# Key, value and query products of two heads as units of 512 and 384 moving columns in a decoder layer

## The chip, the core and the metric

The kernel runs on one core of one Trainium2 chip. The time is device microseconds of one execution. An execution is also profiled: each engine (TensorE is PE, its weight loads PEld, VectorE DVE, ScalarE ACT, GpSimd POOL, SyncE SP) has its instructions recorded with start and length, and the span runs from the first to the last of them.

## The reference

One layer of a hybrid decoder: a normalised and modulated input goes through one large projection, then a recurrent branch and an attention branch with compressed queries and keys run side by side, both are gated by silu, and an output product is added to the input. There are 512 tokens, 2048 model columns and 8 heads. Cut to what matters here:

```
h = rms_norm(x) * (1 + scale) + shift
xr, gr, qc, kvc, kr, ga = split(h @ w_in)              # qc, kvc: 512 columns each
y_rnn = rg_lru_branch(xr, ...) * silu(gr)
q  = (rms_norm(qc,  q_a_norm)  @ w_uq ).reshape(B, S, 8, 128 + 64)    # nope, rope
kv = (rms_norm(kvc, kv_a_norm) @ w_ukv).reshape(B, S, 8, 128 + 128)   # k nope, v
q_nope, k_nope = rms_norm(q_nope), rms_norm(k_nope)    # each head by itself
q_pe = apply_rope(rms_norm(q_pe)); k_pe = apply_rope(rms_norm(kr))
p = softmax(causal((q_nope . k_nope + q_pe . k_pe) / sqrt(192)))
y_att = (p @ v) * silu(ga)
x = x + gate * (concat(y_rnn, y_att) @ w_out)
```

## The kernel before

All matrix products are made in float32 precision from two parts: an operand is split into a high part in a reduced float32 format (a copy on ACT, `act(hi, src, AF.Copy)`) and the rest as low part (a subtraction on DVE), and a product is three matmuls: high by high, high by low, low by high. `wload` (line 192) does this for weights: SP issues the load of a tile into a raw buffer (`wraw`), ACT writes `whi`, DVE writes `wlo`. In the stage of interest there are 6 raw buffers and 3 each of `whi` and `wlo` (`NARROW`, line 30).

The work runs in stages. First come the modulation and the input projection in four chunks of its 2048 rows (tile `pp`, lines 508 to 554), with the recurrent branch beside the last chunk. Of the last chunk, the 8 column blocks of the attention gates (slots `pj24` to `pj31`) are left over. The stage behind it, from about 360 us on, is the attention. It is written as generators that are advanced tick by tick in `ticks` (line 1096):

- `produce(g)` makes q, k and v of the two heads of group g (g = 0 to 3);
- `attend(g)` makes the scores (`sc`), the softmax, the transposes of the probabilities (`tp`) and the product with v (`op`) for the same two heads;
- `fillers` (line 1037) are matmuls that depend on neither: the 8 left-over projection blocks (`pp`, in two loads each), then output products over heads that are done (`oa`).

In each run of `ticks`, `produce(g + 1)` stands beside `attend(g)`, and fillers are strewn between by a quota. This sets priorities. The order within each engine is then fixed at build time by a scheduler that goes by these priorities and by an estimate of when operands are ready; only SP's order is the written one. On the chip every engine takes its instructions strictly in that order, so a matmul whose operand is late holds all that are queued behind it.

`produce` before makes four products per group. `qpe` (line 840) makes the rotary part of q for two heads with the weights as stationary operand and the 512 tokens as moving columns: 12 matmuls of 512 columns into tile `uqp`, a copy, and four transposes (`tqp`, line 851) that bring the tokens into the partitions. Then `unit` (line 786) is used three times, for the other part of q (`wqn`), for k (`wuk`) and for v (`wuv`): a block of 128 tokens is the stationary operand, and 256 columns of weights of two heads move.

```
for b in range(2):
    wh, wl = wload(a[name][g][:, b * S:(b + 1) * S], S)
    for i in range(NT):
        o = pb[i // 2][:, (i % 2) * 256:(i % 2 + 1) * 256]
        for k in (2 * b, 2 * b + 1):
            mm(o, xh[k][:, t], wh[:, c], ...)   # then xh by wl, xl by wh
```

So a load of 512 columns (two of the four row blocks k) serves all four token blocks, 24 matmuls, and a unit has two PSUM banks with two token blocks each. All units share banks 0 and 1 in turn (`BANKS`, kind `u`). `nope` (line 802) takes a whole unit: copies out of both banks (`kt`), sums of squares (`jk`, `hs`), the inverse root on POOL (`rsq`, line 227), the scaling, transposes (`tq`) and the split of the result into `qT` or `kT`. `val` (line 833) copies v into `vt`. The gates' silu is taken in one batch behind the last left-over projection block (lines 1043 to 1046).

Of the kernel before, what the change touches and what calls it, by code (L numbers as in the profile page):

```python
# [12 lines left out]
F32 = mybir.dt.float32  # L13
F32R = mybir.dt.float32r
BF16 = mybir.dt.bfloat16
# [67 lines left out]
def body(ctx, nc, tc, a):  # L83
# [695 lines left out]
    def produce(g):  # L779
# [6 lines left out]
        def unit(name, xh, xl):  # L786
            pb = [bank("u", "u" + name) for _ in range(2)]
            for b in range(2):
                wh, wl = wload(a[name][g][:, b * S:(b + 1) * S], S)
                for i in range(NT):  # L790
                    t = slice(i * P, (i + 1) * P)
                    o = pb[i // 2][:, (i % 2) * 256:(i % 2 + 1) * 256]
                    for k in (2 * b, 2 * b + 1):
                        c = slice((k % 2) * 256, (k % 2 + 1) * 256)
                        mm(o, xh[k][:, t], wh[:, c], k == 0 and i % 2 == 0, False, skip_group_check=True)
                        mm(o, xh[k][:, t], wl[:, c], False, False, skip_group_check=True)
                        mm(o, xl[k][:, t], wh[:, c], False, k == 3, skip_group_check=True)
                if b == 0:
                    yield None
            yield pb  # L800

        def nope(pb, which, grow, dst):
            kt = [p3.tile([P, S], F32, tag="kt", name="kt", bufs=2) for _ in range(2)]
            s = p3.tile([P, 2, 4], F32, tag="hs", name="hs", bufs=2)
            for u in range(2):
                act(kt[u], pb[u], AF.Copy)
            for u in range(2):
                for q in range(4):
                    jk = p3.tile([P, P], BF16, tag="jk", name="jk")
                    act(jk, kt[u][:, q * P:(q + 1) * P], AF.Square, accum_out=s[:, u, q:q + 1])  # L810
            s3 = s.rearrange("p u (i h) -> p (u i) h", h=2)
            rb_ = lambda f: rl[:, which, f, :].rearrange("p (i o) -> p i o", o=1).broadcast_to([P, NT, 2])
            s8 = s.rearrange("p u q -> p (u q)")
            tt(s3, s3, rb_(1), ALU.mult)
            rsq(s8, s8, 1.0 / P, 8)
            tt(s3, s3, rb_(0), ALU.mult)
            yield
            for u in range(2):
                for q in range(4):
                    c = slice(q * P, (q + 1) * P)  # L820
                    stt(kt[u][:, c], kt[u][:, c], s[:, u, q:q + 1], row[:, grow:grow + P], ALU.mult, ALU.mult)
                tp = bank("tq", "tq")
                for d in range(2):
                    for i2 in range(2):
                        q = 2 * i2 + d
                        PE.transpose(tp[:, d * 256 + i2 * P:d * 256 + (i2 + 1) * P], kt[u][:, q * P:(q + 1) * P], ident)  # L826
                for d in range(2):
                    sl = slice(u * 256, (u + 1) * 256)
                    act(dst[d][:, 0, sl], tp[:, d * 256:(d + 1) * 256], AF.Copy)
                    tt(dst[d][:, 1, sl], tp[:, d * 256:(d + 1) * 256], dst[d][:, 0, sl].bitcast(F32), ALU.subtract)  # L830
                yield

        def val(pb):
            for i in range(NT):
                for d in range(2):
                    c0 = (i % 2) * 256 + d * P
                    act(vt4[d][:, i], pb[i // 2][:, c0:c0 + P], AF.Copy, scale=rl[:, 0, 0, i:i + 1])
            yield

        def qpe():  # L840
            wh, wl = wload(a["wqp"][g], S)
            ps = bank("u", "uqp")
            for k in range(4):
                c = slice(k * P, (k + 1) * P)
                mm3(ps, wh[:, c], wl[:, c], qh[k], ql[k], k == 0, k == 3)
            qs = p3.tile([P, S], F32, tag="qa", name="qs")
            act(qs, ps, AF.Copy)
            yield
            tp = bank("tq", "tqp")
            for i in range(NT):  # L850
                PE.transpose(tp[:, i * P:(i + 1) * P], qs[:, i * P:(i + 1) * P], ident)
            o = p3.tile([P, S], F32, tag="qb", name="qo")
            act(o, tp, AF.Square)
# [8 lines left out]
            tt(o8, tp.rearrange("p (n c) -> p n c", n=8), s.rearrange("p (n o) -> p n o", o=1).broadcast_to([P, 8, 64]),  # L862
# [22 lines left out]
        q = qpe()  # L885
        next(q, None)
        pipe.append(q)
        prods.append(q)
        yield
        for name, xh, xl, fin in (("wqn", qh, ql, lambda pb: nope(pb, 1, R_QN, qT)),  # L890
                                  ("wuk", kvh, kvl, lambda pb: nope(pb, 0, R_KN, kT)), ("wuv", kvh, kvl, val)):
            for pb in unit(name, xh, xl):
                if pb is not None:
                    f = fin(pb)
                    next(f, None)
                    pipe.append(f)
                    prods.append(f)
                yield
# [259 lines left out]
def _layout(x, c, positions, w_ada, b_ada, w_in, conv_w, conv_b, w_rg_a, b_rg_a, w_rg_x, b_rg_x, lru_lambda,  # L1158
# [30 lines left out]
    uk = w_ukv[0].reshape(2, 2, P, 4, 2, 2, P)  # L1189
    t = uk.transpose(3, 0, 2, 1, 5, 4, 6)  # L1190
    d["wuk"] = con(t[:, :, :, :, 0].transpose(0, 2, 1, 3, 4, 5)).reshape(4, P, 1024)
    d["wuv"] = con(t[:, :, :, :, 1].transpose(0, 2, 1, 3, 4, 5)).reshape(4, P, 1024)
    uq = w_uq[0].reshape(2, 2, P, 4, 2, 192).transpose(3, 0, 2, 1, 4, 5)
    d["wqn"] = con(uq[..., 0:128].transpose(0, 2, 1, 3, 4, 5)).reshape(4, P, 1024)
    uq2 = w_uq[0].reshape(4, P, 4, 2, 192).transpose(2, 1, 0, 3, 4)
    d["wqp"] = con(uq2[..., 128:192]).reshape(4, P, 512)
# [32 lines left out]
```

## Time and profile before

| | |
|---|---|
| median of 3 runs | 726.15 us (726.0 to 728.82) |
| the profiled execution's own time | 725.46 us |
| its span | 723.7 us |
| TensorE busy, matmuls | 718.7 us, 3608 |
| VectorE busy, instructions | 525.6 us, 945 |
| ScalarE busy, instructions | 354.2 us, 729 |
| granted TensorE clock | 1.00 |
| HBM read, written | 123.11 MB, 4.19 MB |

A row of a group gives line, engine, operation, output and inputs, shapes, count, then busy time and mean length of one, then the engine's idle time ahead of it and who ended most of it. A row of the timeline gives start, length, engine, line, operation, tiles, shape and count, and in brackets the idle time before it and its releaser. The chain is the work that ended last, followed back from the end: at each step to what released it, or to the instruction before it on its engine. All helpers for matmuls, copies and two-operand arithmetic are one line each (123, 88, 116), so tiles' names tell the groups apart. Matmuls overlap: the listed length of one is longer than the distance to the next one's start.

### The profile page before, as it was taken

The page shows a single profiled execution, that of the slowest core. Times are in us where ns is not written, and L with a number is a line of the kernel's source. Part 1 is how long each engine was busy: PE and PEld are TensorE (multiplying, and loading weights), DVE is VectorE, ACT ScalarE, POOL GpSimd, SP SyncE. Part 2 cuts the span into 40 slices and gives each one's busy share as a digit, 9 for nine tenths or more (in the row PEclk, how much of TensorE's full clock was granted, in tenths as well). Part 3 has the DMA queues.
Part 4 walks back from the last instruction along what each step waited for, and adds up shares of the span by engine and source line. Part 5 has one row for each costly group of instructions (what it writes and reads, how often), then busy time and mean ns, then how long its engine had stood idle before and what let it go on. Part 6 is the DMA issues. An engine that isn't in the chain of part 4 may idle for free.

```text
span 723.7 us, 10053 instructions
## 1 busy us (share of the span) xinstructions
PE 718.7 (99%) x3608; PEld 596.0 (82%) x3608; DVE 525.6 (73%) x945; ACT 354.2 (49%) x729; POOL 29.4 (4%) x34
## 2 busy tenths in 40 slices
PE   9999999999999999999999999999999999999998
PEld 4688888888888888888898898898888887888886
DVE  2867999998998889888755566567686786683232
ACT  7277222222233589884455578587465534222221
POOL 0000000000000000001011011111020100000000
PEclk9999999999999999999999999999999999999999
DMA  8998777877613321232342225213334685974330
GB/s 303 408 401 317 297 275 270 352 262 271 241 36 101 108 89 69 90 102 77 93 140 95 81 77 186 71 47 132 125 124 141 219 290 191 318 264 171 115 95 29
DMA packets 46145, 127.95 MB, mean 177 GB/s; under 512 B 5516, under 2 KB 9484, under 8 KB 42512
## 3 DMA queue, kind: packets, MB, share of 16 engines
q1 hardware_dynamic: 39040, 106.35, 41.3%
q10 hardware_dynamic: 7056, 20.97, 8.3%
q8 instruction: 28, 0.46, 0.3%
q14 instruction: 21, 0.17, 0.1%
HBM read 123.11 MB, written 4.19 MB: 176 GB/s over the span
## 4 chain that ended last, share of the span: by engine, by line
PE 99%; DVE 0%; ACT 0%; issue 0%
PE pp L123 48%; PE oa L123 24%; PE sc L123 4%; PE uwuv L123 3%; PE uwqn L123 3%; PE uwuk L123 3%; PE op L123 2%; PE junk_ps L123 2%; PE uqp L123 2%; PE tp L926 1%; PE pk L123 1%; PE tq L826 1%; PE pi L123 1%; PE pr L123 1%; PE tqe L881 0%; PE m_ps L123 0%
## 5 line engine op out<-in xcount | busy, mean ns | idle before, releaser
L123 PE MATMUL pp<-h,whi 128*128 128x512 f32 x992 | 241.1, 390 | 0.0
L88 ACT ACTIVATE whi<-wraw 128x512 fp32r<-128x512 f32 (+4 forms) x172 | 127.0, 741 | 227.7 <-PE pp L123 98.9
L123 PEld LDWEIGHTS pp<-h,whi 128*128 128x128 f32 x992 | 185.1, 188 | 38.3 <-issue 0.4
L116 DVE TENSOR_TENSOR wlo<-wraw,whi 128x512 fp32r<-128x512 f32 (+4 forms) x172 | 141.4, 824 | 72.0 <-ACT whi L88 33.9
L123 PE MATMUL pp<-h,wlo 128*128 128x512 f32 x496 | 126.7, 390 | 0.0
L123 PEld LDWEIGHTS pp<-h,wlo 128*128 128x128 f32 x496 | 92.9, 188 | 19.2
L123 PE MATMUL oa<-yh,whi 128*128 128x512 f32 (+1 forms) x260 | 100.9, 393 | 0.1
L123 PE MATMUL oa<-yl,whi 128*128 128x512 f32 (+1 forms) x260 | 101.0, 389 | 0.0
L116 DVE TENSOR_TENSOR pj<-pp,pj 128x512 f32<-128x512 f32 x96 | 65.0, 689 | 16.6 <-PE pp L123 15.9
L123 PE MATMUL oa<-yh,wlo 128*128 128x512 f32 (+1 forms) x260 | 71.2, 390 | 0.0
L277 DVE CUSTOM_DVE_ANT_0 ada<-ada,cb,vec 128x2048 f32<-128x2048 f32 (+1 forms) x31 | 69.6, 2247 | 1.5 <-DMA ada<-in_ada 1.5
L123 PEld LDWEIGHTS oa<-yl,whi 128*128 128x128 f32 x260 | 49.0, 188 | 9.3 <-DVE yl L116 0.2
L123 PEld LDWEIGHTS oa<-yh,whi 128*128 128x128 f32 x260 | 48.9, 188 | 9.4 <-ACT yh L88 0.3
L123 PEld LDWEIGHTS oa<-yh,wlo 128*128 128x128 f32 x260 | 48.0, 188 | 9.5
L123 PE MATMUL sc<-kT,qT 128*128 128x128 f32 (+3 forms) x96 | 22.5, 331 | 0.0
L918 DVE TENSOR_REDUCE nm<-sc 128x1 f32<-128x128 f32 (+3 forms) x32 | 15.5, 487 | 8.0 <-PE sc L123 7.9
L229 POOL TENSOR_TENSOR hs<-hs,mhalf 128x8 f32<-128x8 f32 x12 | 21.2, 1768 | 1.0
L88 ACT ACTIVATE pr<-sc,nm 128x128 f32<-128x128 f32 (+3 forms) x32 | 16.7, 522 | 9.1 <-DVE nm L918 9.0
L123 PE MATMUL uwuv<-whi,kvt 128*128 128x256 f32 x80 | 20.8, 284 | 0.0
L123 PE MATMUL uwqn<-whi,kvt 128*128 128x256 f32 x80 | 20.7, 286 | 0.0
L277 DVE CUSTOM_DVE_ANT_0 ada<-ada,cbo,modh 128x1024 f32<-128x1024 f32 x16 | 20.5, 1281 | 0.0
L277 DVE CUSTOM_DVE_ANT_0 ada<-ada,cbo,vec 128x1024 f32<-128x1024 f32 x16 | 20.5, 1280 | 0.0
(234 smaller groups left out, 995.8 us busy)
## 6 DMA issues: line engine op xcount, KB each, us to landing
ada<-in_ada SPq DMA_DIRECT2D x28, 1024.0 KB, 7.0
ada<-in_ada ACTq DMA_DIRECT2D x32, 512.0 KB, 5.1
wraw<-in_wout SPq DMA_DIRECT2D x59, 256.0 KB, 3.6
wraw<-in_win SPq DMA_DIRECT2D x22, 512.0 KB, 6.2
wraw<-in_win SPq DMA_DIRECT2D x24, 448.0 KB, 3.2
wraw<-in_win SPq DMA_DIRECT2D x16, 384.0 KB, 5.6
xtok<-in_xtok SPq DMA_DIRECT2D x8, 512.0 KB, 6.6
xo<-in_x SPq DMA_DIRECT2D x16, 256.0 KB, 5.0
```

The costliest lines, as they stand in the source:

```text
L88: return A.activation(out=out, in_=in_, func=func, **kw)
L116: return V.tensor_tensor(out=o, in0=x, in1=y, op=op)
L123: return PE.matmul(out=out, lhsT=lhsT, rhs=rhs, start=start, stop=stop, **kw)
L229: G.tensor_tensor(out=out, in0=out, in1=mhalf[:, :n], op=ALU.pow)
L277: ttr_last[0] = V.tensor_tensor_reduce(out=t, in0=t, in1=cv, op0=ALU.mult, op1=ALU.add, scale=1.0, scalar=vec[:, C_BADA + j:C_BADA + j + 1 ...
L826: PE.transpose(tp[:, d * 256 + i2 * P:d * 256 + (i2 + 1) * P], kt[u][:, q * P:(q + 1) * P], ident)
L918: V.tensor_reduce(out=nm, in_=sp[:, :n], axis=AX.X, op=ALU.max, negate=True)
L926: PE.transpose(tp[:, j * P:(j + 1) * P], pr[:, j * P:(j + 1) * P], ident)
```

## The change

Of the two products of k and v, one is made per group: `wkv`, in which a row block's weights for k and v of both heads stand side by side as 512 moving columns. Both parts of q become one product `wq` with 384 moving columns, 256 for the part without rotation and 128 for the rotary part, so that the rotary part comes out with the tokens in the partitions too and its transposes go. A unit now runs over two pairs of token blocks (u = 0, 1), one bank per token block. A load holds one row block k (384 or 512 columns); for u = 0 four are loaded in the order 0, 1, 2, 3, of which the last two stay split in their buffers, and for u = 1 the order is 3, 2, 1, 0, so that 1 and 0 are loaded again. Within a row block the four matmuls with the high weights come first, then the two with the low ones (for the very first two row blocks of group 0 the high ones of both come first). `nope` and `val` work on one pair of token blocks, and so run twice as often on half as much; their copies out of a bank are 256 or 128 columns wide. `qpe` reads the copy `qs` instead of transposes. A group thus loads 12 tiles (6 of 384 columns, 6 of 512) instead of 7 of 512. `produce` has 8 steps instead of 7, which `ticks` now counts with. The silu of the gates is taken in two batches of four, behind the fifth and the eighth left-over block. The weights are laid out for this on the host ahead of the launch, as they were before.

```diff
-        def unit(name, xh, xl):
-            pb = [bank("u", "u" + name) for _ in range(2)]
-            for b in range(2):
-                wh, wl = wload(a[name][g][:, b * S:(b + 1) * S], S)
...
+        def unit(name, n, xh, xl, fin):
+            held = {}
+
+            def piece(pb, u, ks, kn, ph):
+                k = ks[kn]
+                if k not in held:
+                    held[k] = wload(a[name][g][:, k * n:(k + 1) * n], n)
+                wh, wl = held[k]
+                for i in range(2):
+                    o, t = pb[i][:, :n], cols(2 * u + i)
+                    if ph:
+                        mm(o, xh[k][:, t], wl[:, :n], False, kn == 3)
+                    else:
+                        mm(o, xh[k][:, t], wh[:, :n], kn == 0, False)
+                        mm(o, xl[k][:, t], wh[:, :n], False, False)
+                if ph and u == 0 and kn < 2:
+                    del held[k]
+
             for u in range(2):
+                pb = [bank("u", "u" + name) for _ in range(2)]
+                ks = (0, 1, 2, 3) if u == 0 else (3, 2, 1, 0)
+
+                first = g == 0 and u == 0 and name == "wq"
+                for kn, ph in ((0, 0), (1, 0), (0, 1), (1, 1)) if first else ((0, 0), (0, 1), (1, 0), (1, 1)):
+                    piece(pb, u, ks, kn, ph)
+                yield
+                for kn in (2, 3):
+                    for ph in range(2):
+                        piece(pb, u, ks, kn, ph)
+                for f in fin(pb, u):
+                    next(f, None)
...
+        def nope(pb, u, which, grow, dst):
+            kt = p3.tile([P, S], F32, tag="kt", name="kt", bufs=2)
+            s = p3.tile([P, 4], F32, tag="hs", name="hs", bufs=2)
+            for i in range(2):
+                act(kt[:, i * 256:(i + 1) * 256], pb[i][:, 0:256], AF.Copy)
...
+        def val(pb, u):
+            for i in range(2):
                 for d in range(2):
...
+                    c0 = 256 + d * P
+                    act(vt4[d][:, 2 * u + i], pb[i][:, c0:c0 + P], AF.Copy, scale=rl[:, 0, 0, 2 * u + i:2 * u + i + 1])
+            yield
+
+        def qrope(pb, u):
+            if u == 0:
+                qs.append(p3.tile([P, S], F32, tag="qs", name="qs"))
+            for i in range(2):
+                act(qs[0][:, cols(2 * u + i)], pb[i][:, 256:384], AF.Copy)
+            yield
...
         def qpe():
-            wh, wl = wload(a["wqp"][g], S)
-            ps = bank("u", "uqp")
...
-            for i in range(NT):
-                PE.transpose(tp[:, i * P:(i + 1) * P], qs[:, i * P:(i + 1) * P], ident)
             o = p3.tile([P, S], F32, tag="qb", name="qo")
-            act(o, tp, AF.Square)
+            act(o, qs[0], AF.Square)
...
+        def qfin(pb, u):
+            fs = [qrope(pb, u), nope(pb, u, 1, R_QN, qT)]
+            return fs + [qpe()] if u else fs
+
+        yield from unit("wq", 384, qh, ql, qfin)
+        yield from unit("wkv", 512, kvh, kvl, lambda pb, u: [nope(pb, u, 0, R_KN, kT), val(pb, u)])
...
-            if n == 7:
-                for mm_ in MORDER[24:]:
+            if n in (4, 7):
+                for mm_ in MORDER[24:28] if n == 4 else MORDER[28:]:
...
-            want = -(-7 * (s + 1) // n) if prod is not None else 0
+            want = -(-8 * (s + 1) // n) if prod is not None else 0
```

The order on PE shows the shapes. Before, at the start of k of group 1 (the tiles' numbers tell instances apart; `kvt0`, `lat21` and `kvt1` are parts of the latent of k and v for row blocks 0 and 1):

```order
L123 MATMUL uwuk_3979<-whi_3983,kvt0_1840 128x256
L123 MATMUL uwuk_3979<-wlo_3984,kvt0_1840 128x256
L123 MATMUL uwuk_3979<-whi_3983,kvt0_1840 128x256
L123 MATMUL uwuk_3979<-whi_3983,lat21_2412 128x256
L123 MATMUL uwuk_3979<-wlo_3984,lat21_2412 128x256
L123 MATMUL uwuk_3979<-whi_3983,kvt1_1841 128x256
```

Now, at the start of k and v of group 1, for the two banks `uwkv_4009` and `uwkv_4010`:

```order
L123 MATMUL uwkv_4009<-whi_4013,kvt0_1840 128x512 x2
L123 MATMUL uwkv_4009<-wlo_4014,kvt0_1840 128x512
L123 MATMUL uwkv_4009<-whi_4025,lat21_2412 128x512
L123 MATMUL uwkv_4009<-whi_4025,kvt1_1841 128x512
L123 MATMUL uwkv_4010<-whi_4013,kvt0_1840 128x512 x2
```

Where one weight tile served two row blocks and 24 matmuls, each row block now has a tile of its own (`whi_4013`, `whi_4025`) and six matmuls for this pair of token blocks.

The second place on PE is in group 0, between the two halves of q. `whi_3131` and `whi_3143` (row blocks 2 and 3) are the two that stay for the second half, whose first bank is `uwq_3204`; `pp_3172` is a left-over projection block in two loads, `whi_3175` and `whi_3220`:

```order
L123 MATMUL pp_3172<-h12_1441,whi_3175 128x512 x2
L123 MATMUL uwq_3103<-wlo_3144,lat19_2716 128x384
L123 MATMUL uwq_3104<-wlo_3144,lat19_2716 128x384
L123 MATMUL pp_3172<-h9_1117,wlo_3176 128x512
L123 MATMUL pp_3172<-h10_1185,wlo_3176 128x512
L123 MATMUL pp_3172<-h11_1327,wlo_3176 128x512
L123 MATMUL pp_3172<-h12_1441,wlo_3176 128x512
L123 MATMUL pp_3172<-h13_1570,whi_3220 128x512 x2
L123 MATMUL pp_3172<-h14_1684,whi_3220 128x512 x2
L123 MATMUL pp_3172<-h15_1798,whi_3220 128x512 x2
L123 MATMUL uwq_3204<-whi_3143,lat19_2716 128x384
L123 MATMUL uwq_3204<-whi_3143,kvt4_1844 128x384
```

With two of three high buffers held, the projection's second tile takes the buffer that its first one leaves behind the row at the top; six matmuls lie between that row and its own first use.

The third place, also on PE, is the passage from q to k and v in group 0. `uwq_3204` and `uwq_3205` are the banks of q's second half; `uwkv_3368` takes the bank of `uwq_3204`:

```order
L123 MATMUL uwq_3204<-wlo_3268,kvt2_1842 128x384
L123 MATMUL uwq_3205<-wlo_3268,kvt2_1842 128x384
L123 MATMUL pp_3234<-h13_1570,wlo_3314 128x512
L123 MATMUL pp_3234<-h14_1684,wlo_3314 128x512
L123 MATMUL pp_3234<-h15_1798,wlo_3314 128x512
L123 MATMUL uwkv_3368<-whi_3372,kvt0_1840 128x512 x2
L123 MATMUL uwkv_3368<-wlo_3373,kvt0_1840 128x512
```

Four matmuls stand between the last one into the bank and the next use of it, which waits for two copies on ACT.

More of the change, by code (lines that the diff above doesn't have):

```diff
@@ L784, in produce @@
         grp[g] = (kT, qT, qp, vt4)
-        def unit(name, xh, xl):
-            pb = [bank("u", "u" + name) for _ in range(2)]
-            for b in range(2):
-                wh, wl = wload(a[name][g][:, b * S:(b + 1) * S], S)
-                for i in range(NT):
[L791 to L800, printed above, removed]
@@ L802, in nope @@
-        def nope(pb, which, grow, dst):
-            kt = [p3.tile([P, S], F32, tag="kt", name="kt", bufs=2) for _ in range(2)]
-            s = p3.tile([P, 2, 4], F32, tag="hs", name="hs", bufs=2)
-            for u in range(2):
[L806 to L813, printed above, removed]
+        def unit(name, n, xh, xl, fin):
[14 more added lines that the diff above has]
+                    del held[k]
+            for u in range(2):
+                pb = [bank("u", "u" + name) for _ in range(2)]
[9 more added lines that the diff above has]
+                    next(f, None)
+                    pipe.append(f)
+                    prods.append(f)
+                yield
@@ new lines, in nope @@
+        def nope(pb, u, which, grow, dst):
[3 more added lines that the diff above has]
+                act(kt[:, i * 256:(i + 1) * 256], pb[i][:, 0:256], AF.Copy)
+            for q in range(4):
+                jk = p3.tile([P, P], BF16, tag="jk", name="jk")
+                act(jk, kt[:, q * P:(q + 1) * P], AF.Square, accum_out=s[:, q:q + 1])
+            s3 = s.rearrange("p (i h) -> p i h", h=2)
+            rb_ = lambda f: rl[:, which, f, 2 * u:2 * u + 2].rearrange("p (i o) -> p i o", o=1).broadcast_to([P, 2, 2])
@@ L814, in nope @@
             tt(s3, s3, rb_(1), ALU.mult)
-            rsq(s8, s8, 1.0 / P, 8)
+            rsq(s, s, 1.0 / P, 4)
             tt(s3, s3, rb_(0), ALU.mult)
             yield
[L818 to L822, printed above, removed]
-                for d in range(2):
[L824 to L837, printed above, removed]
-            yield
-        def qpe():
-            wh, wl = wload(a["wqp"][g], S)
-            ps = bank("u", "uqp")
[L843 to L851, printed above, removed]
+            for q in range(4):
+                c = slice(q * P, (q + 1) * P)
+                stt(kt[:, c], kt[:, c], s[:, q:q + 1], row[:, grow:grow + P], ALU.mult, ALU.mult)
@@ new lines, in nope @@
+            tp = bank("tq", "tq")
+            for d in range(2):
+                for i2 in range(2):
+                    q = 2 * i2 + d
+                    PE.transpose(tp[:, d * 256 + i2 * P:d * 256 + (i2 + 1) * P], kt[:, q * P:(q + 1) * P], ident)
+            for d in range(2):
+                sl = slice(u * 256, (u + 1) * 256)
+                act(dst[d][:, 0, sl], tp[:, d * 256:(d + 1) * 256], AF.Copy)
+                tt(dst[d][:, 1, sl], tp[:, d * 256:(d + 1) * 256], dst[d][:, 0, sl].bitcast(F32), ALU.subtract)
@@ L883, in qpe @@
                 yield
[L885 to L898, printed above, removed]
+        def qfin(pb, u):
[3 more added lines that the diff above has]
+        yield from unit("wkv", 512, kvh, kvl, lambda pb, u: [nope(pb, u, 0, R_KN, kT), val(pb, u)])
     def attend(g):
@@ L1188, in _layout @@
     d["wrg"] = g.reshape(8, P, 256)
[L1189 to L1196, printed above, removed]
+    kv = w_ukv[0].reshape(4, P, 4, 2, 2, P)
+    d["wkv"] = con(kv.transpose(2, 1, 0, 4, 3, 5)).reshape(4, P, 2048)
+    uq = w_uq[0].reshape(4, P, 4, 2, 192).transpose(2, 1, 0, 3, 4)
+    parts = [uq[..., 0:128].reshape(4, P, 4, 256), uq[..., 128:192].reshape(4, P, 4, 128)]
+    d["wq"] = con(np.concatenate(parts, axis=-1)).reshape(4, P, 1536)
     d["wlast"] = con(w_out[0][15 * P:, NACC * P:(NACC + 4) * P])
```

4 lines of the change are left out of this document (3 added, 1 removed).

## The prediction

> **What bounds the kernel now.** I read the page first: the busy shares and the chain of work that ended last.
>
> ```profile
> span 723.7 us, 10053 instructions
> PE 718.7 (99%) x3608; PEld 596.0 (82%) x3608; DVE 525.6 (73%) x945; ACT 354.2 (49%) x729; POOL 29.4 (4%) x34
> PE 99%; DVE 0%; ACT 0%; issue 0%
> ```
>
> TensorE is busy 99% of the span and is 99% of the chain. A busy PE can still hide waits, since matmuls are pipelined, so the view of waits for PE comes second: it has one entry, at the kernel's start.
>
> ```profile
> PE junk_ps L123 <- DVE spe L356: 1.6, 1, 1.6
> ```
>
> Third, the table of windows over the stage that the change rewrites, from the first production of q, k, v (about 360 us) to 600 us. After the span's columns come the busy times of PE, its weight loads, DVE, ACT and POOL, then clock, DMA share and GB/s.
>
> ```profile
> 350.00:400.00 50.00, 50.00 (x285) 43.61 (x284) 29.50 (x61) 25.38 (x68) 5.74 (x6) 1.00 0.38 119
> 400.00:450.00 50.00, 50.00 (x320) 44.38 (x318) 30.18 (x75) 35.45 (x93) 3.67 (x4) 1.00 0.37 122
> 450.00:500.00 50.00, 50.00 (x324) 43.99 (x324) 32.20 (x82) 35.04 (x100) 6.88 (x6) 1.00 0.25 84
> 500.00:550.00 50.00, 50.00 (x316) 43.59 (x316) 35.22 (x90) 29.34 (x87) 5.71 (x6) 1.00 0.36 120
> 550.00:600.00 50.00, 50.00 (x276) 42.09 (x276) 39.89 (x85) 24.56 (x72) 3.27 (x2) 1.00 0.67 226
> ```
>
> PE fills all five windows at clock 1.00, while ACT and DVE have 10 to 25 us free in each. So in this stage the time is the sum of what the matmuls cost, start to start, and nothing else ends last. What the change saves on PE comes through whole, as long as ACT and DVE, which split each weight tile into a high and a low part, keep ahead.
>
> **The change, part by part. The matmul shapes.** The price of a matmul is its distance to the next one's start, not its listed duration, which overlaps. The chain in order of time gives it for whole runs (start, length, count):
>
> ```profile
> 55.09 47.60 PE pp L123 x210
> 360.66 2.75 PE uqp L123 x12
> 377.23 2.87 PE uwuk L123 x24
> ```
>
> A matmul of 512 moving columns costs 2.75 / 12 = 0.229 us in the old q part, and 47.60 / 210 = 0.227 in the projection. One of 256 costs 2.87 / 24 = 0.1196. The line through 0.1196 and 0.229 has 0.109 us per 256 columns and 0.010 us left over for each instruction. At 384 it gives 0.174. The trace has 384 columns only in the attention scores; there, in the timeline of PE, and for 512 columns of the same tile (the second row is three matmuls, up to the start of the third row):
>
> ```profile
> 449.66 0.33 PE L123 MATMUL sc<-kst_h,qp 128*128 128x384 f32 x1
> 449.83 0.34 PE L123 MATMUL sc<-kst_l,qp 128*128 128x384 f32 x1
> 450.01 0.23 PE L123 MATMUL sc<-mask_b,ident_b 128*128 128x128 bf16 x1
> ...
> 451.56 0.86 PE L123 MATMUL sc<-kT,qT 128*128 128x512 f32 x3
> 452.26 0.40 PE L123 MATMUL sc<-kst_h,qp 128*128 128x512 f32 x1
> ```
>
> The steps are 0.17 and 0.18 us at 384, and 0.70 / 3 = 0.233 at 512.
>
> Per group of two heads the change removes 3 units of 48 matmuls of 256 columns and 12 matmuls of 512: 144 x 0.1196 + 12 x 0.229 = 19.97 us. It adds 48 of 384 and 48 of 512: 48 x 0.174 + 48 x 0.229 = 19.34. The moving columns are the same, 43,008 both ways, so what is saved is 60 leftovers of 0.010 us: 0.63 us, and 2.5 us over four groups. The bounds are the nearest rows: with 0.17 and 0.227, 19.97 - 19.06 = 0.91 a group, 3.6 in all; with 0.18 and 0.233, 19.97 - 19.82 = 0.15, 0.6 in all. I take 2.5, by the row of the same unit's own 512-column matmuls.
>
> The Trainium skill, page "TensorE: Matmul & The Clock Gate", section "Back-to-back issue gap", gives a warm gap of N / 2.4 + 2.5 ns, so 2.5 ns per matmul over its columns instead of the 10 that the rows show; by it this term would be 4 x 60 x 2.5 ns = 0.6 us. That speaks against the change's main effect; the rows (119.6 ns at 256 columns, where the formula has 109.2) don't agree, and they decide.
>
> **The four transposes.** q's rotary part now comes out with tokens in the partitions, so the four transposes of tile tqp go in each group:
>
> ```profile
> 465.24 0.48 PE L123 MATMUL oa<-yh,whi 128*128 128x512 f32 x1
> 465.56 0.40 PE L123 MATMUL oa<-yl,whi 128*128 128x512 f32 x1
> ...
> 471.76 0.60 PE L851 MATMUL tqp<-row,qs 128*128 128x128 f32 x4
> 472.11 0.36 PE L123 MATMUL sc<-kT,qT 128*128 128x256 f32 x1
> ```
>
> From the first transpose to the next matmul is 0.35 us, 1.4 us over four groups. The first product after another kind of matmul (a transpose, the plain fp32 product with v, the bf16 mask) costs more: 465.56 - 465.24 = 0.32 instead of 0.23. Such entries would be a further saving of 0.09 each if they went, but in the order both kernels have 86 of them behind the last transposes of the rotary key, since other runs are cut more often. So nothing is counted for them, with four either way, 0.4 us, as bound. PE's own saving is 2.5 + 1.4 = 3.9 us, between 1.6 and 5.4.
>
> **Weight tiles.** A group loads 12 tiles instead of 7: per unit four for the first pair of token blocks, of which the last two stay, and two again for the second pair. Every load is one issue on SP, one copy on ACT and one subtraction on DVE:
>
> ```profile
> 360.75 0.53 ACT L88 ACTIVATE whi<-wraw 128x384 fp32r<-128x384 f32 x1 [0.62 <-DVE wlo L116]
> 363.22 0.64 ACT L88 ACTIVATE whi<-wraw 128x512 fp32r<-128x512 f32 x1 [0.68 <-PE uqp L123]
> 373.88 0.60 ACT L88 ACTIVATE kt<-uwqn 128x512 f32<-128x512 f32 x1 [1.59 <-PE uwqn L123]
> 394.44 0.38 ACT L88 ACTIVATE qT<-tq 128x256 fp32r<-128x256 f32 x1 [0.59 <-PE tq L826]
> L88 ACT ACTIVATE vt<-uwuv,rl x32: 355/369/396, 404.2 to 569.9; 128x128 f32<-128x128 f32 x32
> ```
> ```profile
> 363.44 0.56 DVE L116 TENSOR_TENSOR wlo<-wraw,whi 128x384 fp32r<-128x384 f32 x1 [0.18 <-PE uqp L123]
> 364.41 0.69 DVE L116 TENSOR_TENSOR wlo<-wraw,whi 128x512 fp32r<-128x512 f32 x1 [0.41 <-ACT qs L88]
> 372.23 0.17 DVE L116 TENSOR_TENSOR hs<-hs,rl 128x8 f32<-128x8 f32 x1 [1.53 <-POOL hs L229]
> ```
>
> ACT: 7 x 0.64 = 4.5 us a group become 6 x 0.53 + 6 x 0.64 = 7.0. The copies out of PSUM are cut smaller: 4 of 512 columns for kt become 8 of 256 (2.4 to 3.0), and one for q's rotary part becomes four of 128 (0.6 to 1.5, by the row of vt, also a copy of 128 columns out of PSUM). That is 4.1 us more in a group. The fullest window, 35.45 of 50, would stand at about 40. DVE: 7 x 0.69 = 4.8 become 6 x 0.56 + 6 x 0.69 = 7.5, and four more small products of 0.17 make 3.4 us more; its windows with production in them go from 29 to 35 to about 33 to 39. Neither becomes a bound on average, and PE hides all of it. If that cover went, it would be up to 4.1 us a group.
>
> Average room isn't the test; PE takes its instructions in order, and one late tile holds everything queued behind it, the fillers (projection and output products) too. There are three pairs of split buffers, and between the two halves of a unit two of them are held, so one alone turns over. In the order, I took for each tile the PE work (by the prices above) between the last use of the buffer it takes and its own first use. For high parts the least is 2.8 us in before, which left no wait in the trace; now 11 tiles have less, the least 1.26: two matmuls of 384 and four of 512, 0.35 + 0.91 us, ahead of tile whi_3220, which needs a copy of 0.53 in that time. Low parts, which need the subtraction too, have at least 1.9 us where before had 3.6, against 0.53 + 0.56 = 1.1 us. All these suffice if ACT and DVE are free within 0.7 us; at 80% load they sometimes aren't.
>
> **A new wait at the banks.** The second half of a unit writes the two PSUM banks of the first, so its first matmul waits for ACT's copies. The tightest place is in group 0, where only 0.17 + 3 x 0.227 = 0.86 us of PE work lies between the last matmul into a bank of q and the first into it of k and v. ACT must copy 128 and 256 columns there, 0.37 + 0.38 = 0.75, and a start late by some tenths is a wait. All other places have 1.8 us or more. I take 0.4 us for all new waits together: PE has none now, so less than nothing isn't possible, and above I set 2 us, four places of 0.5 us, one such copy or subtraction each that comes in between.
>
> **SP, POOL and the gates' silu.** SP issues five more loads a group, in program order with those of the fillers; bytes a group go from 1.8 to 2.8 MB, where the DMA share in the windows up to 550 us is at most 0.38.
>
> ```profile
> wraw<-in_wout SPq DMA_DIRECT2D x59, 256.0 KB, 3.6
> L229 POOL TENSOR_TENSOR hs<-hs,mhalf 128x8 f32<-128x8 f32 x12 | 21.2, 1768 | 1.0
> 433.42 1.66 ACT L88 ACTIVATE pj<-pj 128x512 f32<-128x512 f32 x3
> 440.07 1.28 ACT L88 ACT_TABLE_LOAD   x1
> ```
>
> A load lands in 3.6 us; the raw buffers reach six loads ahead, in the new order at least 9.5 us of PE work (12.0 before). That hides it; without it one load late is up to 3.6 us. POOL gets two more powers a group of up to 1.77 us; it is busy 7 us of 50 at most. The silus keep their number and five table loads stand behind the latents' part in either order, so they cost nothing: the eight of before, three of them in one piece of 1.66 us, delayed no matmul, and shorter runs delay less.
>
> **The sum.** Against the profiled execution: 725.46 - 3.9 + 0.4 = 722.0 us. The median of the runs shown, 726.15, lies 0.7 above that execution; against it the forecast is 726.15 - 3.5 = 722.6, or 0.48% less. A change of 0.5%, 3.6 us, is about what a measurement of this kernel can tell from none, so the forecast stands almost on that line.
>
> **The rivals.** (1) Collisions eat the gain: at 80% load ACT and DVE are late at a handful of places, 1 to 3 us in all, about 724.3. For it: covers half as long as now, and five more splits a group; against it: even the least cover exceeds the two operations. (2) The new shapes come cheaper than the line, at the projection's 0.227 and at 0.17, with up to four entries fewer: a gain of 4.6 to 5.4 and no wait, about 721.2. For it: the projection's 210 matmuls in a row; against it: the q part's own 0.229. (3) They come dearer, at the scores' 0.18 and 0.233: 1.4 + 0.6 = 2.0 us less, 724.1. The skill's formula for the gap would give the same 0.6 for the shapes. (4) On the other side, the one free buffer pair: if, while two pairs are held, each load has to go copy, subtraction, matmul one after another, behind a queue on ACT, PE stops once in each of the 8 first-to-second-half passages for each of the two loads. It is slower than before once a stop exceeds 3.9 / 16 = 0.24 us. With 0.6 us, one more copy in front, it is 16 x 0.6 - 3.9 = 5.7 us more, 731.9. For it: the held pairs; against it: fillers lie at nearly every such passage. That the change doesn't reach the hardware as written can be left out: the order shows the new shapes.
>
> **How the numbers follow.** Forecast (722.6, own range 722.0 to 723.2) 0.52; rival 1 0.20; rival 2 0.15; rival 3 0.05; rival 4 0.08. The line of 0.5% is at 722.5, so just under half of the forecast's chance, 0.24, lies below it. Faster: 0.24 + 0.15 = 0.39. Same: 0.28 + 0.20 + 0.05 = 0.53. Slower: 0.08. The range runs from 721.0, rival 2's end of 726.15 - 5.1, to 725.7, rival 1 at its 3 us; it leaves out rival 4 and a rest of the others.
>
> **What would show it.** In the new profile: no entry for PE in the view of waits beyond the start, or only tenths; runs of 384 columns at 0.174 us a matmul and of 512 at 0.229 in the chain; about 3.9 us less between the last transposes of the rotary key and the end; ACT near 40 of 50 us in its fullest window. It is wrong if pieces of ACT or DVE appear in the chain between 360 and 600 us, if PE's windows there hold less than 50 us, or if the slopes differ from the line.

## The result and the profile after

The changed kernel takes 722.32 us (median of 6 runs, 722.0 to 723.3), the one before in the same comparison 726.09 us. The ratio is 0.995, with a 95% interval of 0.9938 to 0.9963: 0.5% faster. The interval lies on both sides of the line of 0.5% that the prediction drew between faster and same, so on which side the change falls is not settled.

On the page of the changed kernel the same three lines stand out as before:

```profile
span 721.4 us, 9740 instructions
PE 715.9 (99%) x3352; PEld 585.1 (81%) x3352; DVE 535.0 (74%) x981; ACT 362.0 (50%) x777; POOL 33.7 (5%) x50
PE 99%; DVE 0%; ACT 0%; issue 0%; ACTq 0%
```

256 matmuls are gone: 240 products and 16 transposes, as the shapes say. TensorE still is 99% of span and chain. The view of waits for PE gained one entry, of 0.2 us:

```profile
PE junk_ps L123 <- DVE spe L356: 1.6, 1, 1.6
PE uwkv L123 <- ACT kt L88: 0.2, 1, 0.2
```

In the table of windows (PE, its weight loads, DVE, ACT, POOL, then clock, DMA share, GB/s) PE loses 0.25 us in the first of the five windows from 350 to 600 us and nothing in the other four, of which one is shown:

```profile
350.00:400.00 50.00, 49.75 (x237) 41.90 (x236) 32.39 (x70) 28.25 (x79) 5.87 (x8) 1.00 0.42 131
...
450.00:500.00 50.00, 50.00 (x266) 41.84 (x265) 34.58 (x91) 37.44 (x110) 8.49 (x11) 1.00 0.33 107
```

ACT's fullest window, the one shown second, is 37.44 us; 40 was expected.

**How much of it belongs to the change.** The profiled execution took 723.3 us, 1.0 above the median, and part of that lies ahead of anything that the change touches. So I measure from the start of the rotary key's last transposes to the start of the last output step, first in the timeline of before, then of the changed kernel (start, length, engine):

```profile
342.26 1.03 PE L714 MATMUL ktp<-row,ke 128*128 128x128 f32 x8
343.05 0.94 PE L123 MATMUL pp<-h,wlo 128*128 128x512 f32 x3
...
720.45 0.48 DVE L100 SCALAR_TENSOR_TENSOR xo<-oa,mod,xo 128x256 f32<-128x256 f32 x1 [0.95 <-PE oa L123]
```
```profile
343.11 0.27 PE L714 MATMUL ktp<-row,ke 128*128 128x128 f32 x1
...
717.90 0.48 DVE L100 SCALAR_TENSOR_TENSOR xo<-oa,mod,xo 128x256 f32<-128x256 f32 x1 [0.95 <-PE oa L123]
```

That stretch goes from 378.19 to 374.79 us: 3.40 us less, and the 0.85 us by which this execution came late to it is not the change's. A second profile of the same kernel (below) has 374.81. I use this stretch for every experiment.

**The prices.** The chain of the changed kernel in order of time has runs of the new shapes and, between PE's, pieces of ACT or DVE in three places (360, 377 and 627 us):

```profile
359.61 0.70 DVE pj L116
...
377.43 0.64 ACT whi L88
...
386.36 2.27 PE uwkv L123 x10
...
394.79 2.75 PE uwkv L123 x12
...
473.35 2.11 PE uwq L123 x12
...
626.93 0.70 DVE yt L116
...
627.65 0.64 ACT yh L88
```

A matmul of 384 columns costs 2.11 / 12 = 0.176 us, one of 512 costs 2.27 / 10 = 0.227 to 2.75 / 12 = 0.229. The line gave 0.174 and 0.229.

**The small waits.** A pipelined PE can start late and still be shown as busy, so I compare starts with prices at the chain's ACT and DVE places. In the changed kernel's timeline of PE, the first products of q, the passage from q to k and v, and the last head's output products:

```profile
359.93 1.04 PE L123 MATMUL uwq<-whi,kvt 128*128 128x384 f32 x3
360.81 0.33 PE L123 MATMUL uwq<-whi,lat 128*128 128x384 f32 x1
...
377.53 0.86 PE L123 MATMUL pp<-h,wlo 128*128 128x512 f32 x3
378.56 0.73 PE L123 MATMUL uwkv<-whi,kvt 128*128 128x512 f32 x2 [0.16 <-ACT kt L88]
379.13 0.40 PE L123 MATMUL uwkv<-wlo,kvt 128*128 128x512 f32 x1
...
627.89 0.40 PE L123 MATMUL oa<-yl,whi 128*128 128x512 f32 x1
628.34 1.66 PE L123 MATMUL oa<-yh,whi 128*128 128x512 f32 x6
629.83 0.39 PE L123 MATMUL oa<-yl,whi 128*128 128x512 f32 x1
```

Three matmuls of 384 take 0.88 us from start to start at 359.93, where 3 x 0.176 = 0.53 is the price: 0.35 late. Three of 512 take 1.03 at 377.53 instead of 0.68: 0.35 late, of which the profile shows 0.16 as idle; the two that follow take 0.57 instead of 0.46, 0.11 more. At 627.89 the step is 0.45 instead of 0.23, and the six from 628.34 take 1.49 instead of 1.37: 0.34 late in all, where the chain has `yt` and `yh`. The three places make 1.15 us, of which the view of waits shows 0.2.

What held PE at the first two places stands in the timelines of the changed kernel, of DVE and PE for the first (PE's from 360.3 us on) and of ACT for the second:

```profile
359.61 0.69 DVE L116 TENSOR_TENSOR pj<-pp,pj 128x512 f32<-128x512 f32 x1 [1.29 <-PE pp L123]
```
```profile
360.35 0.62 PE L123 MATMUL uwq<-whi,kvt 128*128 128x384 f32 x2
```
```profile
377.43 0.64 ACT L88 ACTIVATE whi<-wraw 128x512 fp32r<-128x512 f32 x1 [1.68 <-PE pp L123]
377.97 0.26 ACT L88 ACTIVATE qs<-uwq 128x128 f32<-128x128 f32 x1
378.13 0.38 ACT L88 ACTIVATE kt<-uwq 128x256 f32<-128x256 f32 x1
378.39 0.28 ACT L88 ACTIVATE qs<-uwq 128x128 f32<-128x128 f32 x1
```

At 359.61 DVE adds a projection block out of its bank, once PE's last product of that block is done. The product at 360.35 starts 0.05 us after this addition ends and waits for DVE. It is the first one into the second bank of q, and it reads high parts alone, so what it waited for is that bank and not a weight tile. At 377.43 ACT splits a high part, 0.64 us, ahead of the two copies that free the bank for k and v: that is the tight place of 0.86 us that the prediction named.

### The profile page after: what moved, and what is told of

Read it like the earlier page. It is cut to its first block, busy times and chain, and to the rows that moved or that the text cites. A ratio compares the mean times of both kernels' runs of the same rounds, so it can differ in the third digit from the quotient of the medians.

```text
span 721.4 us, 9740 instructions
## 1 busy us (share of the span) xinstructions
PE 715.9 (99%) x3352; PEld 585.1 (81%) x3352; DVE 535.0 (74%) x981; ACT 362.0 (50%) x777; POOL 33.7 (5%) x50
## 4 chain that ended last, share of the span: by engine, by line
PE 99%; DVE 0%; ACT 0%; issue 0%; ACTq 0%
PE pp L123 49%; PE oa L123 24%; PE uwkv L123 6%; PE uwq L123 5%; PE sc L123 4%; PE op L123 2%; PE junk_ps L123 2%; PE tp L934 1%; PE pk L123 1%; PE tq L844 1%; PE pr L123 1%; PE pi L123 1%; PE tqe L897 0%; PE m_ps L123 0%; PE cb_ps L123 0%; PE lps L123 0%
## 5 line engine op out<-in xcount | busy, mean ns | idle before, releaser
L88 ACT ACTIVATE whi<-wraw 128x512 fp32r<-128x512 f32 (+4 forms) x192 | 136.9, 718 | 224.0 <-PE pp L123 104.5
L116 DVE TENSOR_TENSOR wlo<-wraw,whi 128x512 fp32r<-128x512 f32 (+4 forms) x192 | 151.4, 793 | 74.3 <-ACT whi L88 36.6
L123 PE MATMUL uwkv<-whi,kvt 128*128 128x512 f32 x80 | 28.5, 402 | 0.2 <-ACT kt L88 0.2
L229 POOL TENSOR_TENSOR hs<-hs,mhalf 128x4 f32<-128x4 f32 (+1 forms) x20 | 24.8, 1242 | 1.7
L123 PE MATMUL uwq<-whi,kvt 128*128 128x384 f32 x80 | 24.4, 344 | 0.1
L100 DVE SCALAR_TENSOR_TENSOR xo<-oa,mod,xo 128x512 f32<-128x512 f32 (+1 forms) x12 | 8.2, 704 | 17.7 <-PE oa L123 17.7
L88 ACT ACTIVATE jk<-kt 128x128 bf16<-128x128 f32 x64 | 20.9, 327 | 0.6
```

The source lines that it names most:

```text
L88: return A.activation(out=out, in_=in_, func=func, **kw)
L100: return V.scalar_tensor_tensor(out=out, in0=in0, scalar=scalar, in1=in1, op0=op0, op1=op1, **kw)
L116: return V.tensor_tensor(out=o, in0=x, in1=y, op=op)
L123: return PE.matmul(out=out, lhsT=lhsT, rhs=rhs, start=start, stop=stop, **kw)
L229: G.tensor_tensor(out=out, in0=out, in1=mhalf[:, :n], op=ALU.pow)
```

## The experiments

The theory: TensorE's start-to-start time is the end, the change takes 3.9 us of it away, and the collisions that it brings are small. The rivals: shapes worth only 2.5 ns an instruction, splits or held buffers that starve PE, and a silu that matters after all. "The stretch" is the one measured above.

### Only k's and v's products as columns of 256 again

The tiles, loads and banks of the changed kernel stay; each product of 512 columns becomes two of 256, and the scheduler orders the result anew.

```diff
-                    if ph:
-                        mm(o, xh[k][:, t], wl[:, :n], False, kn == 3)
...
+                    for c0, c1 in ((0, 256), (256, 512)) if n == 512 else ((0, n),):
...
+                        if ph:
+                            mm(o[:, c], xh[k][:, t], wl[:, c], False, en, **kw)
```

> The change with every 512-column matmul of k and v cut into two of 256: the same columns, loads, banks and program, 192 matmuls more. Theory (0.010 us per matmul): 192 x 0.010 = 2.0 us and 3 more entries, 0.3: 724.5. Rival (2.5 ns per matmul): 0.5 + 0.3, 723.1. Rival (PE is held by its weight tiles, not by its own work): no change, 722.3.

It took 724.69 us (11 runs; ratio to before 0.9992, 0.9977 to 1.0006). In its chain 24 products in a row stand at the price of the old units:

```profile
439.66 2.87 PE uwkv L123 x24
```

The stretch is 376.63 us, 1.84 more than in the changed kernel, for 192 more matmuls with the same moving columns. Its order has three more entries from another kind of matmul (89 instead of 86), 0.27 us by the prediction's row; between 1.57 and 1.84 us are the matmuls', so 8 to 10 ns each. In this order PE is not late behind the last head, which hides another 0.34 us, so the upper end is nearer. The width of k's and v's products alone is about half of the change's gain, and the price of the rows holds.

### The four transposes back

```diff
+            tp = bank("tq", "tqp")
+            for i in range(NT):
+                PE.transpose(tp[:, i * P:(i + 1) * P], qs[0][:, i * P:(i + 1) * P], ident)
             o = p3.tile([P, S], F32, tag="qb", name="qo")
-            act(o, qs[0], AF.Square)
+            act(o, tp, AF.Square)
```

> The change with the copy of q's rotary part sent through four more transposes per group, each token block by itself, and the transposed copy used for the rest, so that the rotary part of q is wrong in content and the same in size. Theory: 16 transposes at 0.35 / 4 make 1.4 us, 8 more entries 0.7: 724.4. Rival (transposes hide in PE's pipeline): 722.3 to 722.7.

724.64 us (12 runs; 0.999, 0.9976 to 1.0005). The stretch is 376.94 us, 2.15 more. Sixteen transposes at 0.35 us a run of four are 1.4; the order has eight entries more (94), 0.7 us. That sum agrees, but not for the reason expected. Before, the eight `ktp` take 0.79 us up to the next product (342.26 to 343.05) and the four `tqp` 0.35, so each further transpose costs 0.11 us and only the last of a run is followed after 0.02 to 0.03. What the first product behind it costs more, 0.09, is about what the last transpose costs less. So an entry by itself is nearly free, and sixteen transposes are 16 x 0.11 = 1.76 us. The other 0.4 are new waits: by the starts PE is late by about 1.6 us in this run, where the changed kernel has 1.15. The profile shows the largest new one in part, in PE's timeline:

```profile
485.38 0.73 PE L123 MATMUL uwkv<-whi,kvt 128*128 128x512 f32 x2 [0.38 <-ACT kt L88]
```

### A fresh load of every tile in each half

No tile is held for the second half, so the buffer pairs turn over freely and a group loads 16 tiles instead of 12.

```diff
-                if ph and u == 0 and kn < 2:
+                if ph:
                     del held[k]
```

> The change with nothing held: all four row blocks are loaded and split again for the second half, 16 tiles a group instead of 12, and no buffer pair is tied up. Theory (PE bound, splits hidden): 5 more entries, 0.5 us, and perhaps some tenths of waits: 722.8 to 723.4. Rival (ACT and DVE are at the edge, each split more is late): 16 loads more at 0.3 to 0.6 us, 727 to 732. Rival (the held pairs are what starves PE): faster than the change by 0.5 us or more.

722.65 us (8 runs; 0.9961, 0.9947 to 0.9974); the stretch is 374.90, 0.11 more than the changed kernel's. Sixteen more splits in all on ACT and DVE and sixteen more transfers cost a tenth of a microsecond. So ACT and DVE are not at the edge of their load that rival 1 supposed, and the held pairs don't starve PE as rival 4 supposed. The 0.5 us expected for five more entries is not there either, which bears out that an entry by itself costs far less than 0.09 us.

### q's products as 256 and 128 columns

```diff
-                        mm(o, xh[k][:, t], wh[:, :n], kn == 0, False)
...
+                    for c0, c1 in ((0, 256), (256, 384)) if n == 384 else ((0, n),):
```

> The change with every 384-column matmul of q cut into one of 256 and one of 128. Theory, with the scores' row of about 0.112 us for 128 columns: 0.1196 + 0.112 - 0.174 = 0.058 us for each of 192, 11 us, and 12 entries, 1.1: 734. Rival (the line of 0.010 us and 0.109 per 256 columns holds down to 128, 0.065 us): 192 x 0.010 + 1.1 = 3.0 us, 725.3.

735.65 us (5 runs; 1.0147, 1.0125 to 1.0168); the stretch grows by 12.9 us. One row of its chain has the price:

```profile
366.98 2.72 PE uwq L123 x24
```

A pair of 256 and 128 costs 2 x 2.72 / 24 = 0.227 us instead of 0.176. With 0.1196 for the 256, the 128 costs 0.107, nearly as much. The line through 256 and 512 ends somewhere above 128 columns; it must not be drawn on. 192 pairs x 0.051 us are 9.8 us, and the view of waits adds three of 1.5, 0.8 and 0.3 us: in sum 12.4 of the 12.9. Twelve more entries at 0.09, another 1.1, would be too much.

### One batch of silu in the changed kernel

```diff
-            if n in (4, 7):
-                for mm_ in MORDER[24:28] if n == 4 else MORDER[28:]:
+            if n == 7:
+                for mm_ in MORDER[24:]:
```

> The change with the gates' silu in one batch, as before. Theory: the silu is hidden; only the order shifts, with 90 entries instead of 86, 0.4 us: 722.3 to 722.9. Rival (the two batches take a burst of ACT off the path of the weight tiles): more than 1 us slower than the change, 723.5 or more.

724.49 us (11 runs; 0.9988, 0.9976 to 1.0); the stretch is 376.82, 2.0 us more than with two batches. The prediction, and my expectation here, had no cost for it. In the timeline of this kernel, ACT and then PE:

```profile
424.89 1.28 ACT L88 ACT_TABLE_LOAD   x1
426.18 3.75 ACT L88 ACTIVATE pj<-pj 128x512 f32<-128x512 f32 x7
429.84 1.44 ACT L88 ACTIVATE whi<-wraw 128x384 fp32r<-128x384 f32 x3
```
```profile
430.40 0.97 PE L123 MATMUL uwq<-whi,kvt 128*128 128x384 f32 x4 [1.86 <-ACT whi L88]
```

A table load and seven silus keep ACT for 5 us, and the splits of q's weight tiles queue behind them. PE waits 1.86 us for the first. With two batches the same table load is followed by three silus (1.67 us in the changed kernel), since four were done one by one beside the projection. So the second batch belongs to the change: without it 2 of its 3.4 us would be lost.

### Two batches of silu in the kernel before

```diff
-            if n == 7:
-                for mm_ in MORDER[24:]:
+            if n in (4, 7):
+                for mm_ in MORDER[24:28] if n == 4 else MORDER[28:]:
```

> The kernel before with the gates' silu in two batches and nothing else changed; its order has the same 86 entries. Theory (the batch of eight holds weight tiles back only where they are loaded one row block at a time): 0 within 0.3 us, 726. Rival (the two batches by themselves make the 2 us that undoing them cost): 724.

730.36 us (6 runs; 1.0061, 1.0045 to 1.0077): slower by 0.6%, where no difference was expected. The stretch, from the fastest of the six runs (728.51), is 381.09, 2.9 more than before's. The longest of the new waits for PE:

```profile
PE op L123 <- ACT PT L88: 0.7, 1, 0.7
PE tp L926 <- ACT PT L88: 0.5, 1, 0.5
```

With two more of 0.2 us they make 1.6 us in four places, none of them at a silu: they lie in the attention, behind other work of ACT. By the starts the same places and one beside them come to 2.8 us, so the 2.9 are waits. The batch changes no matmul, yet the order behind it came out differently on every engine. Why the new order has these waits and the old one none was not settled.

### The k and v unit alone, and the q unit alone

Each is built on the kernel before, with one of the new units and the two batches of silu.

```diff
-        for name, xh, xl, fin in (("wqn", qh, ql, lambda pb: nope(pb, 1, R_QN, qT)),
...
+        for pb in unit2("wqn", qh, ql):
...
+        yield from unit("wkv", 512, kvh, kvl, lambda pb, u: [nope(pb, u, 0, R_KN, kT), val(pb, u)])
```

> k and v as in the change, q as before. Theory (each matmul costs its columns plus 0.010 us, so fewer and wider ones save the leftovers; PE is never starved): 96 x 0.1196 - 48 x 0.229 = 0.49 us a group, 2.0 in all; its order has 80 entries from another kind of matmul instead of 86, 0.5 us more; so 726.1 - 2.5 = 723.6. Rival (the shapes are worth 2.5 ns a matmul, the gain comes from elsewhere): 0.5 + 0.5 less than before, 725.1. Rival (the extra loads starve PE): above 726.

730.07 us (5 runs; 1.0058, 1.0046 to 1.0071): the half of the change that has most of the saved matmuls makes the kernel slower. The stretch is 381.95, 3.8 more than before's. Its waits, then the first of the three places in the timelines of ACT and PE:

```profile
PE uwkv L123 <- ACT vt L88: 4.2, 3, 1.5
```
```profile
448.31 0.38 ACT L88 ACTIVATE qT<-tq 128x256 fp32r<-128x256 f32 x1 [0.80 <-PE tq L891]
448.60 0.65 ACT L88 ACTIVATE kt<-uwkv 128x256 f32<-128x256 f32 x2
449.12 1.16 ACT L88 ACTIVATE vt<-uwkv,rl 128x128 f32<-128x128 f32 x4
```
```profile
439.51 0.61 PE L123 MATMUL uwkv<-wlo,lat 128*128 128x512 f32 x2
...
447.67 0.61 PE L891 MATMUL tq<-row,kt 128*128 128x128 f32 x4
...
449.82 0.50 PE L123 MATMUL uwkv<-whi,lat 128*128 128x512 f32 x1 [1.43 <-ACT vt L88]
```

This is the wait at the banks that the prediction described, at a size it only allowed for: six copies empty the two banks of the first half, and the second half's first product waits for the last of them, once in each of groups 1 to 3. PE has work enough in between: 42 matmuls in this place, from 439.51 us on. But in ACT's queue the copies stand behind one of q's transposes (`qT`), which waits for PE's `tq` at 447.67, and so they start 8 us after the banks were filled. In the same group of the changed kernel the copies begin at 443.99, right behind the last products into the banks (443.56 us); 23 matmuls between the halves are enough there, and none waits. So the mechanism is real, costs 1.4 us a place where it bites, and the changed kernel is spared by its order on ACT; that is luck, since the prediction looked at what PE has in between and not at this queue.

```diff
+        def qfin(pb, u):
+            fs = [qrope(pb, u), nope(pb, u, 1, R_QN, qT)]
+            return fs + [qpe()] if u else fs
...
+        yield from unit("wq", 384, qh, ql, qfin)
+        for name, xh, xl, fin in (("wuk", kvh, kvl, lambda pb: nope2(pb, 0, R_KN, kT)), ("wuv", kvh, kvl, val)):
```

> q as in the change, k and v as before. Theory: 48 x 0.1196 + 12 x 0.229 - 48 x 0.174 = 0.14 us a group, 0.5 in all, and 1.4 from the 16 transposes that go, less 8 more entries at 0.09, 0.7: 726.1 - 1.2 = 724.9. Together with the other half the two gains should come to that of the change within 0.5 us, once the entries are set off. Rival (silu batches or the order of the fillers make the gain): both halves alone give nearly nothing or nearly all.

725.8 us (11 runs; 1.0004, 0.9995 to 1.0013), no difference; the stretch is 378.39. The saved transposes are paid back behind the last head, as its chain shows:

```profile
628.97 1.27 DVE ada L277
...
630.25 0.61 DVE yt L116
...
630.89 0.64 ACT yh L88
...
631.57 1.66 PE oa L123 x6
```

The last gated output `yt` stands behind a piece of 1.27 us in DVE's queue, and PE waits 1.5 us for its high part. So the two halves give +4.1 us and 0 where the whole gives -3.8: with the waits in them, the parts don't add.

### More split buffers, and one more step of output products

Five raw, four high and four low buffers instead of six, three and three:

```diff
-NARROW = (6, 3, 3)
+NARROW = (5, 4, 4)
```

> The change with four split buffers each for high and low parts instead of three, and five raw buffers instead of six to make room. Theory (waits of PE are some tenths, so there is little to win): 4 entries fewer, 0.4, and up to 0.4 us of waits: 721.5 to 722.3. Rival (the one free buffer pair costs several waits that hide in the lengths of matmuls): 1.5 us or more faster, below 721.

723.27 us (7 runs; 0.9965, 0.9952 to 0.9978), not the 721.5 to 722.3 expected. The wait at 378 us is gone, and a larger one is there, in PE's timeline:

```profile
629.79 1.88 PE L123 MATMUL oa<-yh,whi 128*128 128x512 f32 x7 [1.44 <-ACT yh L88]
```

In this order no product stands between the last head's `op` and the first use of `yh`. I then gave that place more to do, with one more step of output products kept for it:

```diff
-NARROW = (6, 3, 3)
+NARROW = (5, 4, 4)
...
-NPOST = 2
+NPOST = 3
```

> The change with four split buffers of each part and five raw ones, and with three output products instead of two set ahead of the last head's product. Theory: the waits that the change has left (0.3 us at the bank of group 0, 0.3 us behind the last head) go, and the 1.4 us wait behind the last head of the run with four buffers goes too; 4 entries fewer, 0.4: about 1 us below the change, 721.3. Rival (the waits are not on the path, only the matmuls' sum is): 0.4 below the change, 721.9.

723.17 us over five runs (0.996, 0.9946 to 0.9974), not the 721.3 expected. A sixth, the profiled one, took 1463.68 us, so its trace can't be set beside the others, and where the rest went stays open. The same two edits in the kernel before:

> The kernel before with the buffers and output products of the fastest version. Theory: there are no waits to take away, 5 entries fewer, 0.4 us: 725.6. Rival (buffers and tail are what gains, whatever the shapes): as much as they bring to the change, 725 or less.

733.9 us (6 runs; 1.0109, 1.0093 to 1.0124), 8 us slower than before, and not the 725.6 expected. In its view of waits PE stands once for 1.5 us at `tp`, for a copy `PT`, and twice, 1.0 us together, at `tq`, for `qp`, both on ACT. More buffers don't help by themselves; another order comes with them, and it is worse here.

### The changed kernel again

> The change once more, beside the others: 3.4 to 3.8 us below the kernel before, ratio 0.995.

722.87 us (6 runs; 0.9955, 0.9941 to 0.9968), the stretch 374.81 against 374.79. The stretch repeated within 0.02 us this once, so I read differences of some tenths between these profiles. No version was faster than the change.

## Why the prediction held, and where it didn't

**The bound** was read rightly: PE stays at 99%, and what left PE's queue left the time, less the new waits.

**The shapes** were priced rightly. 384 columns measured 0.176 us (0.174 from the line), 512 measured 0.227 to 0.229. Undoing the width of k and v gives 8 to 10 ns a matmul, where the rows gave 10. The Trainium skill's formula in "TensorE: Matmul & The Clock Gate", section "Back-to-back issue gap", N / 2.4 + 2.5 ns, which that section gives for an isolated matmul, would give 0.5 us for those 192 matmuls; the measured 1.6 to 1.8 doesn't agree with it here.

**The transposes** were priced short, with the right sum within the bounds. From the first of four to the next product is 0.35 us, but the prediction took this for the price of all four and kept the entry apart. With as many entries in both orders, sixteen transposes fewer save 1.76 us and not 1.4, as the run that has them back shows. The parts, 1.6 to 1.8 for k and v, 1.76 for the transposes and 48 x 0.010 = 0.5 for q, which no run isolates, make 3.9 to 4.1.

**Weight tiles**: the fear was larger than the thing. ACT grew by 362.0 - 354.2 = 7.8 us, not 4 x 4.1 = 16.4; DVE by 9.4, not 13.6. The step that failed is that listed durations of neighbours overlap: on ACT a copy of 128 columns is followed after 0.16 us and one of 256 after 0.26 (377.97, 378.13, and 378.39 for the next), though they are listed at 0.26 and 0.38. 48 more instructions on ACT then took 0.16 us each. And four more loads a group cost 0.1 us in all.

**New waits**: the named place was right, its kind too (a split on ACT ahead of the copies), but the term of 0.4 us was too small. Starts late by 0.35 at the first unit, 0.46 at the bank and 0.34 behind the last head make 1.15 us. Two signs that the prediction named against itself are there, though small: pieces of DVE and ACT in the chain at 360 and 377 us, and a window of 49.75. Two of the places were not in the prediction: it looked at the weight buffers and at the banks that q, k and v hand to each other, not at a bank that a projection block leaves, nor at the way from the last `op` through `yt` and `yh` to the output products. Nor was before free of waits, as the view of waits had it. In its timeline, the like place behind an `op` is

```profile
609.93 0.28 PE L926 MATMUL tp<-row,pr 128*128 128x128 f32 x1
610.30 0.98 PE L123 MATMUL oa<-yh,whi 128*128 128x512 f32 x3
611.12 0.38 PE L926 MATMUL tp<-row,pr 128*128 128x128 f32 x2
611.48 0.50 PE L123 MATMUL oa<-yl,whi 128*128 128x512 f32 x1
```

0.37 us for one transpose and 0.36 for two, where 0.03 and 0.14 are the price: 0.34 and 0.22 late, 0.56 together. So PE's own saving is 3.40 + 1.15 - 0.56 = 4.0 us, where the parts give 3.9 to 4.1 and the prediction had 3.9, and the new waits cost 0.6 net instead of 0.4: the net of 3.4 against 3.5 is close because both terms are.

**The silu** is the step that was wrong: "they cost nothing", since "shorter runs delay less". In the two kernels as they stand the term holds, for neither trace has PE waiting behind a silu, but the reason doesn't. It rests on "three of them in one piece of 1.66 us", which is the end of a longer run that a window of the timeline had cut. In before's ACT timeline from 430 us on it is

```profile
430.55 1.28 ACT L88 ACT_TABLE_LOAD   x1
...
432.38 2.70 ACT L88 ACTIVATE pj<-pj 128x512 f32<-128x512 f32 x5
```

A table load and six silus keep ACT for 4.5 us, nearly the 5 of the single batch in the changed kernel. There it costs 2.0 us and here nothing, so its length is not what decides, but what stands behind it. In the changed kernel three splits for q queue behind it, each for six products of 0.176 us, 1.06 us, where a tile of the old units fed 2.87; the two batches avoid it. That the smaller tiles are what makes the batch dear was argued, not tried apart. In the kernel before, two batches cost 2.9 us, at other places. So what the batches do depends on what else is in the order, and that the changed kernel had two was luck for the forecast: with one it would have been 724.5 us, above its range.

**The rivals**: collisions (1) came in part, 1.15 us, and half as much was there before. Cheaper (2) and dearer (3) shapes put 3.6 and 0.6 us on the shapes, where 2.1 to 2.3 are measured, with 0.5 of it from the slopes. The starving buffers (4) fall by the run that holds none. Stops at the banks as long as rival 4's do exist, three of 1.4 us, but in the kernel with k and v alone.

## What to carry to other kernels

Where PE never waits, price matmuls from start to start and make few wide ones of many narrow ones before anything else; below some width, here between 128 and 256 columns, a narrower one is hardly cheaper. Price transposes together with the product behind them: taken up to its start alone, they look too cheap. Where the order of all engines is made by a scheduler, any edit can deal new waits, of up to 8 us here, so test the whole and each part, and judge an edit by waits that repeat, not by the sum of its parts. Look for them in the queues of ACT and DVE too: a copy that frees a bank can stand behind one that waits for PE. Put a batch on ACT where PE has work for the batch's own length ahead of the weight tiles behind it. And ask a timeline with a window wider than the run that you read from it.

## What the runs showed of the hardware

- A matmul of 128 columns with weights of its own costs 0.107 us, nearly as much as one of 256 (0.1196).
- At a passage from transposes to these products the first product takes about 0.09 us more, and the last transpose is followed after 0.03 us where two transposes lie 0.11 apart; together the passage costs next to nothing. Five more entries in the run that loads all tiles came with 0.11 us in all.
- An idle time that the profile shows for PE leaves out what the modelled end of the matmul before covers: 0.16 us shown at 378.56, 0.35 by the starts.
